# Two transformer blocks on one core: the gate of out_proj multiplied in from PSUM, affine steps behind the last tile, bias tables negated on ScalarE

## The chip, the core and the metric

The kernel runs on one core of a Trainium2 chip. The core has five engines with an instruction queue each, and each queue runs strictly in order: TensorE (PE) multiplies matrices into PSUM, VectorE (DVE) and ScalarE (ACT) work on tiles in SBUF and PSUM, GpSimd (POOL) on tiles in SBUF, and SyncE (SP) issues most of the DMAs. Engines wait for each other through semaphores. The metric is the device time of one execution in microseconds (us); lower is better. "Layer 0" and "layer 1" are the two layers of the second block.

## What is computed

Two transformer blocks run one after the other, all in float32. The first has 512 tokens of width 1024 and holds dilated attention, an mLSTM, cross attention and a mixture of experts; the change touches nothing there. The second block takes its output x (512 latent tokens) and 256 context tokens through two layers. Cut to what matters:

```python
for l in range(2):
    sh1, sc1, g1, sh2, sc2, g2 = split(silu(c) @ w_ada[l] + b_ada[l], 6)
    u = x * (1 + sc1) + sh1                # (the context has modulations of its own)
    o = concat(neighborhood_attention(u, bias from na_rpb[l]),   # 6 heads
               gated_linear_attention(u),                        # 4 heads, both directions
               gqa_attention(u))                                 # 6 query, 2 key heads
    x = layer_norm(ALPHA * x + g1 * (o @ w_out[l]), ln1_g[l], ln1_b[l])
    v = x * (1 + sc2) + sh2
    x = layer_norm(ALPHA * x + g2 * (silu(v @ wa) * (v @ wb)) @ w_ffn_out[l], ln2_g[l], ln2_b[l])
```

In the first layer the context goes through the same steps, ahead of the latent tokens. A layer_norm is a normalisation ((x - mean) / std) and an affine step (times ln_g, plus ln_b).

## The kernel before

Each float32 product is made of three matmuls: both operands are split into a high and a low part (names ending in _h and _l). A weight chunk of 256x512 or 1024x128 is loaded by SP into one of four buffers `raw`; ACT casts it to w_h (L350), DVE subtracts (L351) to get w_l, and PE multiplies it with the tokens (mm3, L343). Three split chunks (w) can stand ready. In places a chunk first takes a gate: `wchunk` with a `row` lets POOL multiply raw by it (L387).

The 512 latent tokens are four tiles of 128. A layer runs gated linear attention (GLA, with the decay tables glD made on POOL and exponentials on ACT), the projections, neighbourhood attention (NA), grouped-query attention (GQA), `out_proj` and `ffn`. In NA the keys of a head pair (nak) are duplicated by SBUF-to-SBUF DMAs (L533) before PE can make scores (sc, L542), and each head has a bias table `nab`, loaded by a DMA that POOL issues (L1621) and negated by POOL (L1622). Two nab buffers are used in turn.

`out_proj` multiplies the attention's output by W_out, gated by g1b on POOL, in two halves of 512 columns. DVE adds ALPHA * x (L2077) and takes the statistics (bn_stats, L2048). When a tile's second half is done, `done1` normalises it: `ln_moments` runs a reciprocal square root as a chain of one-column DVE instructions (L462 to L476, named rqv, rqz, rqa, rqb), DVE scales the tile (L2059), PE transposes it (tp, L500), ACT applies the modulation and casts (ht, hTf_h), DVE makes the low part (hTf_l, L515), and POOL brings x itself through the affine step for the residual (`affine`, L2066 and L2067: two instructions of 128x1024). ln_g and ln_b are folded into the modulation columns of the transposed copy, so that copy does not wait for POOL. `ffn` takes g2b into w_ffn_out on POOL (66 chunks, L387). Its last product ends tile by tile in `done2`, which is built like `done1` and in layer 0 also stores x to DRAM (xd, SP). In layer 1 `last` ends a tile: for tiles 0 to 2 DVE normalises and POOL does the affine step, for tile 3 DVE does all of it in three instructions (L2323, then L2326 twice) and the store goes out in halves.

The order of the instructions on each engine is set by the framework's scheduler, which simulates the queues while the program is built; memory of closed pools is reused behind semaphores. A change of one instruction can therefore move others on all engines, SP's queue among them. SP's DMAs carry semaphores in turn (DMAHW0 to DMAHW7), and one waits until the DMA that had the same one before has landed.

Of the kernel before, what the change touches and what calls it, by code (L numbers as in the profile page):

```python
# [9 lines left out]
F32 = mybir.dt.float32  # L10
# [5 lines left out]
OP = mybir.AluOpType  # L16
# [4 lines left out]
P = 128  # L21
D = 1024
KT = 8
T1 = 512
# [211 lines left out]
def f32(ap):  # L236
    return ap.bitcast(F32)
# [22 lines left out]
class Kern:  # L260
# [1351 lines left out]
    def na_bias(self, l, pool, bias):  # L1612

        h = len(bias)
        if h < NA_H:
            if h < 2:
                t = pool.tile([P, 4, 256], F32, name=f"nab{h}")
                self.nc.gpsimd.memset(t[:, 3, :], 0.0)
            else:
                t = bias[h - 2]  # L1620
            self.nc.gpsimd.dma_start(out=t[:, 0:3, :].rearrange("p a c -> p (a c)"), in_=self.A["nabias"][l, h])  # L1621
            self.nc.gpsimd.tensor_scalar_mul(t[:, 0:3, :], t[:, 0:3, :], -1.0)  # L1622
            bias.append(t)

    def na(self, l, hT, T, W, ctxd, full, d, vd, pool, pool0, g0, begun, bias):
# [430 lines left out]
    def ln_core(self, t, st):  # L2056

        m, r = self.ln_moments(st)
        self.nc.vector.tensor_scalar(out=t, in0=t, scalar1=m, scalar2=r, op0=OP.subtract, op1=OP.mult)  # L2059

    def call(self, f):
        if f is not None:
            f()
# [5 lines left out]
    def out_proj(self, l, oT, nt, x, g1b, pool, tile_done):  # L2069

        nc = self.nc
        W = self.A["w_out_2"][l]
        stats = {}

        def ev(i, c0, n, ps):
            s = slice(c0, c0 + n)
            nc.vector.scalar_tensor_tensor(out=x[:, i, s], in0=x[:, i, s], scalar=ALPHA, in1=ps[:, :n], op0=OP.mult, op1=OP.add)  # L2077
            self.ln_stats(stats, x, i, c0)
            if c0 + n == D:
                return tile_done(i, stats[i])  # L2080
        if nt < 4:
            return self.proj_tok(oT, nt, W, lambda *a: self.call(ev(*a)), row=g1b)
        self.proj_tok(oT, nt, W[:, 0:512], ev, row=g1b)
        self.proj_last(oT, nt, W, ev, pool, KT, g1b, (512,))

    def ffn(self, l, hT, T, x, g2b, pool, tile_done):

# [47 lines left out]
    def layer2(self, l, st, ctxd, full, last=None, keep_hT=False):  # L2135
# [3 lines left out]
        nt = T // P  # L2139
# [62 lines left out]
        with tpool("xx") as px:  # L2202
            x = px.tile([P, nt, D], F32, name="x")
            nc.sync.dma_start(out=x, in_=st["xd"].rearrange("(t p) d -> p t d", p=P))
            wk = px
            s, t = self.mod_cols(cols_, 4, 3, j, self.c("vpack", f"ln1_g{l}"), self.c("vpack", f"ln1_b{l}"), f"mc{j}", self.cst)
            hTf = self.hl_tile(px, [P, KT, T], "hTf")
            with tpool("l2") as lp:
                if not lat:
                    gr, lg, lb = ln_rows(lp)  # L2210

                def done1(i, stats):
                    self.ln_core(x[:, i, :], stats)

                    def rest():
                        self.hT_tile(x[:, i, :], i, hTf, s, t, lp, () if lat else (0, 2))
                        self.affine(x[:, i, :], x[:, i, :], lg, lb)
                    return rest
                self.out_proj(l, oT, nt, x, gr, wk, done1)
            oes.close()  # L2220
            st["hes"].close()
            with tpool("l3") as lp:
                gr = lp.tile([P, D], F32, name="g2b")
                self.ada_bcast(rows, 5, j, gr)
                lg, lb = (self.bcast_row(lp, r + 4 * l, n) if j == 0 else None for r, n in ((4, "lng"), (5, "lnb")))
                if last is None:
                    self.core_tile(st, nt)
                    hTn = st["hT"]
                    s2, t2 = self.mod_cols(st["ada"][l + 1][1], 1, 0, j, self.c("vpack", f"ln2_g{l}"),
                                           self.c("vpack", f"ln2_b{l}"), f"md{j}", self.cst)  # L2230

                    xd = self.dr.tile([T, D], F32, name=f"xd{l}{j}") if j == 0 else None

                def done2(i, stats):
                    if last is not None:
                        return last(i, x[:, i, :], stats, lg, lb)
                    self.ln_core(x[:, i, :], stats)

                    def rest():
                        self.hT_tile(x[:, i, :], i, hTn, s2, t2, lp, () if lat else (0, 2))  # L2240
                        if xd is not None:
                            self.affine(x[:, i, :], x[:, i, :], lg, lb)
                            nc.sync.dma_start(out=xd[i * P:(i + 1) * P, :], in_=x[:, i, :])
                    return rest
                self.ffn(l, lambda k: hTf[:, k, :], T, x, gr, wk, done2)
                if last is None:
                    st["xd"] = xd
        return d
# [18 lines left out]
    def main_stream(self):  # L2267
# [46 lines left out]

        def last(i, x, stats, g, b):
            rows = self.out[i * P:(i + 1) * P, :]
            if i < 3:
                self.ln_core(x, stats)
                self.affine(x, x, g, b)
                nc.sync.dma_start(out=rows, in_=x)  # L2320
                return
            m, r = self.ln_moments(stats)
            nc.vector.scalar_tensor_tensor(out=x, in0=x, scalar=m, in1=g, op0=OP.subtract, op1=OP.mult)  # L2323
            for c in range(0, D, 512):
# [26 lines left out]
```

## Time and profile before

| | us |
|---|---|
| three timed runs | 2722.61, 2729.33, 2729.94 (median 2729.33) |
| the profiled execution | 2717.65 |
| its span | 2715.8 |
| busy: PE / DVE / ACT / POOL | 2501.9 / 1747.8 / 1272.7 / 490.9 |

PE's granted clock is 0.96 of full speed over the span. The stages of the second block's latent tokens lie at these times of the span: GLA, projections and NA of layer 0 to about 1455, GQA to 1545, out_proj to 1603, FFN 0 to 1960, its norm and the start of layer 1 to 2000, NA of layer 1 at 2120 to 2195, GQA to 2270, out_proj to 2336, FFN 1 to 2690, the last norm to 2711.

How to read it: a row of a timeline has start, duration, engine, line, operation, the tile written and the tiles read; a bracket at its end tells how long the engine stood idle before and what ended that. An instruction's duration includes the time in which it is held up by another engine at memory. A table of windows gives each engine's busy time in a stretch.

### The profile page before, as it was taken

How to read it: one execution, taken by the hardware profiler on the slowest of the kernel's cores; microseconds unless marked ns; L12 is line 12 of the kernel's file. 1: busy time of each engine (PE TensorE's matmuls, PEld its weight loads, DVE VectorE, ACT ScalarE, POOL GpSimd, SP SyncE). 2: the span in 40 equal slices, each digit the busy share in tenths (PEclk: the TensorE clock that was granted, in tenths of full speed). 3: DMA queues.
4: the chain of work that ended last, by engine and by line, in shares of the span. 5: the costliest groups of instructions: out<-in, count | busy, mean ns of one | idle time of the engine just before them, and what ended most of it. 6: DMA issues, size and time to landing. Idle time of an engine off the chain costs nothing.

```text
span 2715.8 us, 35914 instructions
## 1 busy us (share of the span) xinstructions
PE 2501.9 (92%) x13176; PEld 1953.3 (72%) x13176; DVE 1747.8 (64%) x3095; ACT 1272.7 (47%) x2375; POOL 490.9 (18%) x335
## 2 busy tenths in 40 slices
PE   8999899898979999979988999999989789999997
PEld 5547575676658888867875588888778556888885
DVE  3346646887687787787777564444677676644446
ACT  4343444567755555556646532222356474422221
POOL 1100000201121111112223031111243220411103
PEclk9999899898989999989989999999989899999998
DMA  7765357589767888766352323333323424233331
GB/s 273 210 202 172 109 197 243 167 277 297 270 224 258 270 261 292 255 200 208 98 144 92 112 76 98 95 93 94 95 82 119 124 77 132 82 97 94 93 93 55
DMA packets 354723, 436.53 MB, mean 161 GB/s; under 512 B 20336, under 2 KB 228080, under 8 KB 354544
## 3 DMA queue, kind: packets, MB, share of 16 engines
q1 hardware_dynamic: 350128, 416.90, 48.7%
q0 software_dynamic: 4416, 17.30, 1.9%
q8 instruction: 105, 1.72, 0.3%
q14 instruction: 74, 0.61, 0.1%
HBM read 387.21 MB, written 38.01 MB: 157 GB/s over the span
## 4 chain that ended last, share of the span: by engine, by line
PE 52%; DVE 14%; DMA 5%; issue 5%; ACT 4%; POOL 1%; DVEq 0%; SPq 0%; ACTq 0%; POOLq 0%
PE fab L343 20%; PE pj L343 17%; DVE w_l L351 4%; PE pf L343 3%; PE oat L635 3%; PE h L343 3%; ACT w_h L350 2%; PE yps L343 2%; PE ptp L575 1%; DMA raw<-in_w 1%; DVE rqa L468 1%; PE sc L542 1%; DMA raw<-in_w_ffn_out 1%; POOL raw L387 1%; DMA nak_h<-nak_h 1%
## 5 line engine op out<-in xcount | busy, mean ns | idle before, releaser
L351 DVE TENSOR_TENSOR w_l<-raw,w_h 128x1024 fp32r<-128x1024 f32 (+2 forms) x530 | 696.3, 1325 | 451.5 <-ACT w_h L350 442.9
L350 ACT CAST w_h<-raw 128x1024 fp32r<-128x1024 f32 (+2 forms) x530 | 527.2, 1007 | 844.6 <-PE fab L343 271.0
L343 PE MATMUL fab<-hTf_l,w_h 128*128 128x512 f32 (+1 forms) x1104 | 386.6, 351 | 3.6 <-DVE hTf_l L515 3.6
L343 PE MATMUL fab<-hTf_h,w_h 128*128 128x512 f32 (+1 forms) x1104 | 385.9, 351 | 2.0 <-ACT hTf_h L514 1.7
L343 PE MATMUL fab<-hTf_h,w_l 128*128 128x512 f32 (+1 forms) x1104 | 386.5, 350 | 0.8 <-DVE w_l L351 0.7
L387 POOL TENSOR_TENSOR raw<-raw,g2b 128x1024 f32<-128x1024 f32 x66 | 171.0, 2595 | 756.8 <-DMA raw<-in_w_ffn_out 680.0
L343 PE MATMUL pj<-w_l,hT_h 128*128 128x512 f32 (+3 forms) x608 | 227.6, 375 | 9.9 <-DVE w_l L351 9.9
L343 PEld LDWEIGHTS fab<-hTf_l,w_h 128*128 128x128 f32 x1104 | 209.1, 189 | 35.7 <-DVE hTf_l L515 4.0
L343 PEld LDWEIGHTS fab<-hTf_h,w_h 128*128 128x128 f32 x1104 | 208.6, 189 | 35.3 <-ACT hTf_h L514 2.9
L343 PEld LDWEIGHTS fab<-hTf_h,w_l 128*128 128x128 f32 x1104 | 209.2, 189 | 33.4 <-DVE w_l L351 1.7
L343 PE MATMUL pj<-w_h,hT_h 128*128 128x512 f32 (+3 forms) x608 | 219.8, 374 | 10.4 <-ACT w_h L350 5.2
L343 PE MATMUL pj<-w_h,hT_l 128*128 128x512 f32 (+3 forms) x608 | 224.3, 371 | 0.0
L343 PE MATMUL pj<-w_h,wk_h 128*128 128x512 f32 x376 | 146.9, 396 | 6.1 <-DVE x L2096 4.5
L343 PE MATMUL pj<-w_l,wk_h 128*128 128x512 f32 x376 | 148.6, 396 | 1.2 <-DVE w_l L351 1.2
L343 PE MATMUL pj<-w_h,wk_l 128*128 128x512 f32 x376 | 145.8, 395 | 0.9 <-DVE wk_l L351 0.9
L343 PEld LDWEIGHTS pj<-w_h,hT_h 128*128 128x128 f32 x608 | 117.8, 196 | 38.4 <-ACT w_h L350 8.4
L343 PEld LDWEIGHTS pj<-w_l,hT_h 128*128 128x128 f32 x608 | 118.7, 195 | 36.8 <-DVE w_l L351 14.2
L343 PE MATMUL pf<-hT_h,w_h 128*128 128x512 f32 (+3 forms) x376 | 133.1, 355 | 9.1 <-DVE nak_l L351 4.0
L343 PEld LDWEIGHTS pj<-w_h,hT_l 128*128 128x128 f32 x608 | 119.1, 196 | 21.9 <-issue 5.4
L343 PE MATMUL pf<-hT_h,w_l 128*128 128x512 f32 (+3 forms) x376 | 130.8, 348 | 0.0
L343 PE MATMUL pf<-hT_l,w_h 128*128 128x512 f32 (+3 forms) x376 | 130.3, 347 | 0.0
L577 ACT COPY pT<-ptp 128x512 f32<-128x512 f32 (+3 forms) x184 | 88.5, 497 | 72.7 <-PE ptp L575 71.8
(594 smaller groups left out, 4928.1 us busy)
## 6 DMA issues: line engine op xcount, KB each, us to landing
raw<-in_w SPq DMA_DIRECT2D x192, 512.0 KB
raw<-in_w_ffn_in SPq DMA_DIRECT2D x132, 512.0 KB
raw<-in_w_ada SPq DMA_DIRECT2D x96, 512.0 KB
raw<-in_w_in SPq DMA_DIRECT2D x76, 512.0 KB
raw<-in_w_ffn_out SPq DMA_DIRECT2D x66, 512.0 KB
raw<-in_w_out SPq DMA_DIRECT2D x32, 512.0 KB
yd<-ysb SPq DMA_DIRECT2D x16, 512.0 KB
raw<-in_w_in SPq DMA_DIRECT2D x16, 384.0 KB
```

The lines of the kernel that those rows point to most:

```text
L343: self.nc.tensor.matmul(out, lhsT=l, rhs=r, start=first and k == 0 and i == 0, stop=last and k == n - 1 and i == 2, **kw)
L350: nc.scalar.copy(out=hl.hi, in_=src)
L351: nc.vector.tensor_sub(out=hl.lo, in0=src, in1=f32(hl.hi))
L387: self.nc.gpsimd.tensor_tensor(out=raw, in0=raw, in1=row.unsqueeze(1).to_broadcast([P, kt, n]), op=OP.mult)
L468: nc.vector.scalar_tensor_tensor(out=a, in0=z, scalar=v, in1=z, op0=OP.mult, op1=OP.mult)
L542: self.nc.tensor.matmul(o, lhsT=q, rhs=k.hi, start=True, stop=False)
L575: self.behind = nc.tensor.transpose(tp[:, b * P:(b + 1) * P], st["p"][:, (b0 + b) * P:][:, :P], self.ident)
L577: nc.scalar.copy(out=pT()[:, slice(b0, b0 + bb), ts], in_=tp[:, :bb * P].rearrange("p (b t) -> p b t", t=P))
L635: self.nc.tensor.matmul(st["o"][64 * hh:64 * hh + 64, cols_], lhsT=v(hh), rhs=pT(hh), start=n == 0, stop=n == len(terms) - 1, skip_group_c ...
```

## The change

- `na_bias`: the negation of the twelve nab tables moves from POOL to ACT.
- `out_proj` for the latent tokens: W_out is no longer multiplied by g1b on POOL. DVE multiplies the product by g1b from PSUM into a tile gps (128x512), and the residual add reads gps in place of PSUM.
- `done1` and layer 0's `done2`: the affine steps of the four latent tiles, and the stores to xd, no longer follow each tile. They are collected and issued behind a one-column POOL copy (bhd) that reads the last column of the last tile's low part, so that POOL starts them once the last tile is transposed and split.
- `last`: all four tiles now end on DVE, as tile 3 did, with stores in halves.

```diff
     def na_bias(self, l, pool, bias):
-            self.nc.gpsimd.tensor_scalar_mul(t[:, 0:3, :], t[:, 0:3, :], -1.0)
+            self.nc.scalar.mul(t[:, 0:3, :], t[:, 0:3, :], -1.0)
...
+    def behind_input(self, hT, pool, works):
+
+        t = pool.tile([P, 1], F32, name="bhd", tag="bhd", bufs=1)
+        with self.tc.issue_after(self.nc.gpsimd.tensor_copy(t, f32(hT.lo[:, KT - 1, T1 - 1:T1])).ins):
+            for f in works:
+                f()
...
         def ev(i, c0, n, ps):
             s = slice(c0, c0 + n)
+            if nt == 4:
+                t = pool.tile([P, 512], F32, name="gps", tag="gps", bufs=1)
+                nc.vector.tensor_tensor(out=t, in0=ps, in1=g1b[:, s], op=OP.mult)
+                ps = t
             nc.vector.scalar_tensor_tensor(out=x[:, i, s], in0=x[:, i, s], scalar=ALPHA, in1=ps[:, :n], op0=OP.mult, op1=OP.add)
...
-        self.proj_tok(oT, nt, W[:, 0:512], ev, row=g1b)
-        self.proj_last(oT, nt, W, ev, pool, KT, g1b, (512,))
+        self.proj_tok(oT, nt, W[:, 0:512], ev)
+        self.proj_last(oT, nt, W, ev, pool, KT, None, (512,))
...
-                        self.affine(x[:, i, :], x[:, i, :], lg, lb)
+                        later.append(lambda: self.affine(x[:, i, :], x[:, i, :], lg, lb))
+                        if not lat:
+                            later.pop()()
...
+                if lat:
+                    self.behind_input(hTf, lp, later)
...
-                            self.affine(x[:, i, :], x[:, i, :], lg, lb)
-                            nc.sync.dma_start(out=xd[i * P:(i + 1) * P, :], in_=x[:, i, :])
+                            later.append(lambda: keep_x(i))
...
+                def keep_x(i):
+                    self.affine(x[:, i, :], x[:, i, :], lg, lb)
+                    nc.sync.dma_start(out=xd[i * P:(i + 1) * P, :], in_=x[:, i, :])
...
+                if later:
+                    self.behind_input(st["hT"], lp, later)
...
         def last(i, x, stats, g, b):
             rows = self.out[i * P:(i + 1) * P, :]
-            if i < 3:
-                self.ln_core(x, stats)
-                self.affine(x, x, g, b)
-                nc.sync.dma_start(out=rows, in_=x)
-                return
             m, r = self.ln_moments(stats)
```

What this does to the queues is seen in the orders of the built programs. Names carry buffer numbers, and a bracket names the semaphores that an instruction waits for.

POOL in the norm behind FFN 0, before: from the last weight multiply on, each tile's multiply by ln_g (L2066) and add of ln_b (L2067).

```order
L387 TENSOR_TENSOR raw_18076<-raw_18076,g2b_15843 128x1024 [waits DMAHW7_49,DMAHW4_49,DVE_49]
L2066 TENSOR_TENSOR x_15397<-x_15397,lng_15846 128x1024 [waits DVE_49,PE_49]
L2067 TENSOR_TENSOR x_15397<-x_15397,lnb_15848 128x1024 [waits Pool_49]
L2066 TENSOR_TENSOR x_15397<-x_15397,lng_15846 128x1024 [waits DVE_49,PE_49] x2
L2067 TENSOR_TENSOR x_15397<-x_15397,lnb_15848 128x1024 [waits Pool_49] x2
```

POOL at the same place, now:

```order
L387 TENSOR_TENSOR raw_18086<-raw_18086,g2b_15853 128x1024 [waits DMAHW7_49,DMAHW4_49,DVE_49]
L2064 COPY bhd_18363<-hT_l_15864 128x1 [waits DMASW6_49,DVE_49]
L2073 TENSOR_TENSOR x_15397<-x_15397,lng_15856 128x1024 [waits PE_49] x4
L2074 TENSOR_TENSOR x_15397<-x_15397,lnb_15858 128x1024 [waits Pool_49] x4
L1737 TENSOR_TENSOR tcq_19611<-cpack_66,vpack_67 128x256
```

The pairs that were released tile by tile now stand as four multiplies and four adds behind bhd, and the tables of layer 1 (tcq and what follows) stand behind all eight.

SP in the neighbourhood attention of layer 1, before: the duplicated keys of the second head pair (nak), the context's values (navc) and the context's keys of the third (nakc).

```order
L1659 DMA navc_19864<-nav1256_12147 128x2x128 [waits DMAHW5_49]
L533 DMA nak_h_19866<-nak_h_19866 64x512 [waits DMAHW6_49,Activation_49]
L533 DMA nak_l_19867<-nak_l_19867 64x512 [waits DMAHW7_49,DVE_49]
L1659 DMA navc_20098<-nav1256_12147 128x2x128 [waits DMAHW0_49]
L533 DMA nak_h_19866<-nak_h_19866 64x512 [waits DMAHW1_49,Activation_49]
L533 DMA nak_l_19867<-nak_l_19867 64x512 [waits DMAHW2_49,DVE_49]
L375 DMA nakc_h_20370<-nakc12_h_12412 128x512 [waits DMAHW3_49,PE_49]
L375 DMA nakc_l_20372<-nakc12_l_12414 128x512 [waits DMAHW4_49,PE_49]
```

SP at the same place, now:

```order
L1659 DMA navc_19876<-nav1256_12147 128x2x128 [waits DMAHW5_49]
L533 DMA nak_h_19878<-nak_h_19878 64x512 [waits DMAHW6_49,Activation_49]
L1659 DMA navc_20110<-nav1256_12147 128x2x128 [waits DMAHW7_49]
L375 DMA nakc_h_20382<-nakc12_h_12412 128x512 [waits DMAHW0_49,PE_49]
L533 DMA nak_l_19879<-nak_l_19879 64x512 [waits DMAHW1_49,DVE_49]
L375 DMA nakc_l_20384<-nakc12_l_12414 128x512 [waits DMAHW2_49,PE_49]
L533 DMA nak_h_19878<-nak_h_19878 64x512 [waits DMAHW3_49,Activation_49]
L533 DMA nak_l_19879<-nak_l_19879 64x512 [waits DMAHW4_49,DVE_49]
```

The two nakc loads moved ahead of the second nak_h and nak_l, which now wait for DMAHW3 and DMAHW4.

ACT at the start of layer 1, before: casts of weight chunks (w_h), the first GLA products (glr, glq), the scaled queries of two groups (glqb) and the gates (gla_a).

```order
L350 CAST w_h_18580<-raw_18578 128x1024 [waits DMAHW1_49,PE_49]
L1840 COPY glr_18381<-pf_18400 32x512 [waits PE_49]
L350 CAST w_h_18610<-raw_18608 128x1024 [waits DMAHW2_49,PE_49]
L1868 ACTIVATE glq_18568<-pf_18401 128x512 [waits PE_49]
L1971 ACTIVATE glqb_18786<-glq_18568,cpack_66 128x2x128 [waits Activation_49,Pool_49]
L1971 ACTIVATE glqb_18786<-glq_18568,cpack_66 128x2x128 x2
L1971 ACTIVATE glqb_18800<-glq_18568,cpack_66 128x2x128 [waits DVE_49]
L1971 ACTIVATE glqb_18800<-glq_18568,cpack_66 128x2x128 x2
L350 CAST w_h_18640<-raw_18638 128x1024 [waits DMAHW3_49,PE_49]
L1850 ACTIVATE gla_a_18548<-glz_18550,vpack_67 128x512 [waits PE_49]
```

ACT at the same place, now:

```order
L350 CAST w_h_18592<-raw_18590 128x1024 [waits DMAHW1_49,PE_49]
L350 CAST w_h_18622<-raw_18620 128x1024 [waits DMAHW2_49,PE_49]
L350 CAST w_h_18652<-raw_18650 128x1024 [waits DMAHW3_49,PE_49]
L1840 COPY glr_18393<-pf_18412 32x512
L1868 ACTIVATE glq_18580<-pf_18413 128x512
L1971 ACTIVATE glqb_18798<-glq_18580,cpack_66 128x2x128 [waits Activation_49,Pool_49]
L1971 ACTIVATE glqb_18798<-glq_18580,cpack_66 128x2x128 x2
L1971 ACTIVATE glqb_18812<-glq_18580,cpack_66 128x2x128 [waits Pool_49]
L1971 ACTIVATE glqb_18812<-glq_18580,cpack_66 128x2x128 x2
L1850 ACTIVATE gla_a_18560<-glz_18562,vpack_67 128x512 [waits PE_49]
```

Three chunk casts now stand ahead of GLA's work, and both glqb groups wait for POOL: the counts in the built program are that of the fourth multiply for the first group and that of the fourth add for the second. The cast of the fourth chunk, which stood eight rows behind gla_a, now stands behind the decay tables' exponentials, where the cast of the fifth stood.

## Rows read from the trace of the kernel before

**Rows 1.** The page: busy time, share of the span and instructions by engine.
```profile
PE 2501.9 (92%) x13176; PEld 1953.3 (72%) x13176; DVE 1747.8 (64%) x3095; ACT 1272.7 (47%) x2375; POOL 490.9 (18%) x335
```
**Rows 2.** POOL's groups by shape: out<-in xcount | busy us, mean ns | idle before, releasers.
```profile
L387 POOL TENSOR_TENSOR raw<-raw,g1b 128x1024 f32<-128x1024 f32 x24 | 60.1, 2524 | 232.0 <-DMA raw<-in_w_out 152.8 <-DMA g1b<-adard 18.7 <-issue 15.8
L2067 POOL TENSOR_TENSOR x<-x,lnb 128x1024 f32<-128x1024 f32 x17 | 42.8, 2521 | 1.2
...
L1622 POOL TENSOR_SCALAR nab<-nab 128x768 f32<-128x768 f32 x12 | 26.9, 2249 | 47.9 <-DMA nab<-in_nabias 47.9
```
**Rows 3.** DVE timeline in the norm behind out_proj 0: start us, us, instruction.
```profile
1570.29 0.22 DVE L468 SCALAR_TENSOR_TENSOR rqa<-rqz,rqv 128x1 f32<-128x1 f32 x1
...
1571.38 0.81 DVE L2059 TENSOR_SCALAR x<-x,bmv,rqz 128x1024 f32<-128x1024 f32 x1
...
1577.23 2.25 DVE L468 SCALAR_TENSOR_TENSOR rqa<-rqz,rqv 128x1 f32<-128x1 f32 x1
```
**Rows 4.** POOL timeline of the same stretch: the second affine step of two tiles.
```profile
1577.06 2.40 POOL L2067 TENSOR_TENSOR x<-x,lnb 128x1024 f32<-128x1024 f32 x1
...
1584.43 2.40 POOL L2067 TENSOR_TENSOR x<-x,lnb 128x1024 f32<-128x1024 f32 x1
```
**Rows 5.** Windows: length, busy us by engine, PEclk, DMA share, GB/s.
```profile
1455.00:1490.00 35.00, 24.98 (x158) 16.76 (x156) 31.70 (x68) 25.14 (x64) 17.20 (x7) 0.90 0.33 109
1500.00:1545.00 45.00, 40.81 (x209) 23.39 (x208) 24.69 (x76) 27.94 (x82) 0.00 (x0) 1.00 0.20 64
...
2188.00:2220.00 32.00, 22.57 (x138) 14.79 (x132) 28.91 (x55) 21.38 (x53) 17.20 (x7) 0.84 0.31 102
...
1575.00:1603.00 28.00, 23.83 (x152) 20.81 (x151) 23.62 (x40) 14.84 (x38) 18.70 (x8) 1.00 0.08 19
1603.00:1940.00 337.00, 337.00 (x1471) 272.92 (x1470) 158.63 (x147) 90.97 (x109) 55.92 (x22) 0.99 0.34 101
```
**Rows 6.** PE timeline: the scores behind the duplicated keys, layer 0 and layer 1.
```profile
1421.69 0.55 PE L542 MATMUL sc<-nak_h,naq 128*128 128x256 f32 x1 [8.00 <-DMA nak_h<-nak_h]
...
2148.95 0.55 PE L542 MATMUL sc<-nak_h,naq 128*128 128x256 f32 x1 [12.61 <-DMA nak_h<-nak_h]
```
**Rows 7.** SP timeline in layer 1's neighbourhood attention: DMA issues.
```profile
2140.84 0.55 SPq L533 DMA_DIRECT2D nak_l<-nak_l  x1
...
2147.31 0.34 SPq L375 DMA_DIRECT2D nakc_l<-nakc_l  x1
```
**Rows 8.** PE's waits from 1575 to 1603: us in total, times, longest.
```profile
PE fab L343 <- DVE hTf_l L515: 1.8, 1, 1.8
PE tp L500 <- DVE x L2059: 1.7, 3, 0.8
```
**Rows 9.** PE's waits from 1958 to 1990.
```profile
PE tp L500 <- DVE x L2059: 10.8, 2, 5.9
```
**Rows 10.** DVE timeline behind FFN 0: first and last of five blocked instructions.
```profile
1960.14 2.00 DVE L473 SCALAR_TENSOR_TENSOR rqz<-rqa,rqz 128x1 f32<-128x1 f32 x1
...
1976.89 2.80 DVE L2059 TENSOR_SCALAR x<-x,bmv,rqz 128x1024 f32<-128x1024 f32 x1
```
**Rows 11.** ACT timeline at layer 1's start: the first glqb and the fifth chunk's cast.
```profile
1999.27 2.51 ACT L1971 ACTIVATE glqb<-glq,cpack 128x256 f32<-128x256 f32 x6
...
2015.91 1.03 ACT L350 CAST w_h<-raw 128x1024 fp32r<-128x1024 f32 x1
```
**Rows 12.** PE timeline there: the first products of the first and the fourth chunk.
```profile
2002.40 0.50 PE L343 MATMUL pj<-w_h,hT_h 128*128 128x512 f32 x1
...
2019.23 0.40 PE L343 MATMUL pj<-w_h,hT_h 128*128 128x512 f32 x1
```
**Rows 13.** DVE's groups from 2680 to 2716, the last norm.
```profile
L468 DVE SCALAR_TENSOR_TENSOR rqa<-rqz,rqv 128x1 f32<-128x1 f32 x8 | 10.2, 1280 | 0.2
...
L2323 DVE SCALAR_TENSOR_TENSOR x<-x,bmv,lng 128x1024 f32<-128x1024 f32 x1 | 2.5, 2549 | 0.0
...
L2326 DVE SCALAR_TENSOR_TENSOR x<-x,rqz,lnb 128x512 f32<-128x512 f32 x2 | 1.4, 750 | 0.0
```

More of the change, by code (lines that the diff above doesn't have):

```diff
@@ L2208, in layer2 @@
             with tpool("l2") as lp:
+                later = []
                 if not lat:
@@ L2241, in rest @@
                         if xd is not None:
-                            self.affine(x[:, i, :], x[:, i, :], lg, lb)
-                            nc.sync.dma_start(out=xd[i * P:(i + 1) * P, :], in_=x[:, i, :])
-                    return rest
+                            later.append(lambda: keep_x(i))
+                    return rest
+                def keep_x(i):
+                    self.affine(x[:, i, :], x[:, i, :], lg, lb)
+                    nc.sync.dma_start(out=xd[i * P:(i + 1) * P, :], in_=x[:, i, :])
+                later = []
                 self.ffn(l, lambda k: hTf[:, k, :], T, x, gr, wk, done2)
+                if later:
+                    self.behind_input(st["hT"], lp, later)
                 if last is None:
```

## The prediction

> **What bounds the kernel now.** The engine totals come first: TensorE (PE) is busy for 92% of the span, VectorE (DVE) for 64% [rows 1], so only PE's pauses can be won. POOL's groups tell what POOL does: the gate on W_out, the affine steps and the negated bias tables take 2.2 to 2.5 us an instruction, and the negations also waited 47.9 us for their loads [rows 2]. The DVE and POOL timelines show the coupling: one Newton step of the reciprocal root (L468) takes 0.22 us alone and 2.25 us where POOL's affine step of 2.40 us lies over it [rows 3, 4]. The stage table shows where PE pays [rows 5]. It is full for all of FFN 0, where POOL multiplies weights 22 times, and loses 4.2 us of 28 in the norm behind out_proj 0; layer 1 repeats that. In the 35 us in which layer 0's gate multiplies run, PE is busy for 71%, and for 91% in the attention right behind them; in layer 1's 32 us it is 71% too. So POOL costs time where DVE sets PE's pace, and nothing where PE is full.
>
> **Gate out of W_out.** 16 POOL instructions of 2.52 us go (of 24; the context's 8 stay) [rows 2]. If those 35 and 32 us ran at the later attention's 40.81 of 45, they would take 27.5 and 24.9 us: 7.5 and 7.1 us less is the upper bound [rows 5]. Not all of that idling is POOL's, since the windows also hold the change from one attention to the next; I take 2 a layer as the lower bound, a third of it. Nothing shows which end is nearer, so I take 5 each: **-10** (-4 to -14). W_out's casts now need no POOL and stand earlier on ScalarE (ACT) and DVE, inside neighbourhood attention, whose PE stalls below cover them. The gate returns as 16 DVE multiplies of 128x512 from PSUM, at most 0.75 us each by the two-input step of that shape [rows 13]; that is counted in the norm term.
>
> **Negation on ACT, and the queue that moves with it.** 12 multiplies of 128x768 on ACT cost at most a 128x1024 cast, 1.03 us [rows 11], by width 0.8: 9.5 us on an engine that is busy for 47% [rows 1]. ACT now also waits, in order, for the loads that POOL waited for; softmax exponentials and the casts of the keys (nak) are queued behind. What hides this are PE's two long stalls on the keys' duplicating DMAs, 8.0 us in layer 0 and 12.6 in layer 1 [rows 6], which lie behind such waits in each layer; without them each wait would cost what it lasts. I take 0 (to +3).
> The scheduler also reorders SP's queue. In layer 1 the loads nakc_h and nakc_l (256 KB each) now stand ahead of the second nak_h and nak_l. In the order listing those two take over the semaphore names DMAHW3 and DMAHW4 that the nakc loads had, so they wait for the same earlier transfers. The second nak_l was issued at 2140.84, nakc_l at 2147.31 [rows 7]; PE went on at 2148.95, when the keys had landed [rows 6]. So nak_l may go out 6.5 us later, with less traffic ahead of it: 0 to 6.5, of which I take the middle, 3. Layer 0 swaps one such load: 1 (0 to 2.5). Together **+4** (0 to 9).
>
> **The norm behind out_proj.** PE's waits there are 1.7 us for the normalised x in three pieces and 1.8 us for the last hTf_l [rows 8], within the 4.2 us of idling [rows 5]. With the affine steps behind the last tile, a tile loses about 2.2 us of blocked DVE time and gains a multiply of 0.75; DVE's period falls from the 7.4 us between two tiles' affine steps [rows 4] to some 5.9, just under PE's own 23.83 us for four tiles [rows 5]. What is late next is the last tile's transposes and casts, which stay: about 0.9 us. 4.2 - 0.9 = 3.3 a layer: **-6.6** (-3 to -8.4). The deferred run of 8 x 2.45 = 20 us then lies over FFN's start, beside its weight splits. What hides it is the ring of three split chunks, as it hides FFN 0's 22 POOL multiplies at 337 of 337 us [rows 5]; without that cover each split could wait 2.4 us.
> Here a rule speaks against the change. The Trainium skill (SBUF — State Buffer, Who interferes with whom) says that a VectorE instruction with two SBUF inputs contends with a GpSimd instruction that reads SBUF, and whichever comes second blocks for the whole instruction. Rows 3 and 4 agree, 0.22 against 2.25 us. By the rule the new residual add, which reads the gated product from SBUF and no longer from PSUM, becomes one more victim; with POOL empty there, the sum is the same by both.
>
> **The norm behind FFN 0, and layer 1's start.** Here PE waits 10.8 us for the normalised x [rows 9]. On the chain to the last x five DVE instructions are blocked; the first and the last take 2.00 and 2.80 us, all five 11.3 [rows 10], and alone they would take about 1.6 (four of 0.2, one of 0.8 [rows 3]): 9.7 us. But I do not book that. In the order listing ACT's second group of glqb, and DVE's, wait for POOL, by the built program's count for the last of the eight affine steps, since they reuse the affine rows' memory; behind them on ACT stand the gate activations, the decay's exponentials and the cast of the fourth weight chunk. Before, glqb at 1999.27 found POOL's steps long done [rows 11]. Now the last x ends near 1979.7 - 9.7 = 1970; its transposes, copies and splits take about 6 us (estimate), and 20 us of POOL end at 1996, or 1998 if DVE stretches them. The fourth cast stands where the fifth stood, 16.6 us behind glqb (2015.91 [rows 11]), so it runs at about 2013 to 2015, and PE has its chunk at about 2016. Before, PE began the first chunk at 2002.40 and the fourth at 2019.23 [rows 12]. It now comes to the fourth 9.7 us earlier, at 2009.5, and waits some 7 us: **-3**, nearest to the rows of ACT (+2 to -9.7).
> The reordered xd stores on SP wait for the same POOL steps; the fourth chunk's load stands ahead of them, and the loads behind are needed later.
>
> **The last norm.** After FFN 1 DVE alone sets the end; its chain is full from PE's last products on. Eight L468 take 10.2 us instead of 1.8, L2323 takes 2.5 instead of the 1.4 of two L2326 [rows 13], and three L2059 of 0.8 [rows 3] go: -11.9. Three tiles take on an L2323 and two halves, 3 x (1.4 + 1.4) = +8.4. **-3.5** (-2 to -5).
>
> **Sum.** -10 + 4 - 6.6 - 3 - 3.5 = -19.1 us: from the profiled execution's 2717.65 to 2698.6 (its span and the 1.9 us around it alike). That run lies 11.7 us under the median of the three timed runs, so the forecast takes the same step from the median: 2729.3 - 19.1 = **2710 us**. With the terms' bounds partly cancelling, its own range is 2702 to 2719.
>
> **Rivals.**
> - The wait for POOL does not bind (chance 0.20): the affine run ends sooner or PE has other work, and the FFN norm brings its 9.7. For it: PE's 10.8 us of waiting is real. Against it: the order of ACT. 2710 - 6.7 = 2703 us.
> - The attention is not held by POOL (0.22): its idle time is the change between the two attentions, and the gate brings 2 a layer. For it: the windows hold that change too. Against it: the two windows' equal 71% around the same POOL work. 2710 + 6 = 2716 us.
> - Slower (0.08): ACT takes over POOL's 47.9 us of waiting for the bias loads [rows 2] with the exponentials queued behind. If all but the two stalls of 8.0 and 12.6 us [rows 6] reaches PE, that is +27.3: 2710 + 27.3 = 2738 us. It turns the result from 19 us of uncovered waits on. Against it: ACT is busy for half of the time only, and the first two tables of a layer are loaded before the attention begins.
> - The forecast keeps 0.50.
>
> **How the numbers follow.** About 0.3% (8 us) is what a measurement of this kernel can tell from no change, so faster is below 2721 and slower above 2737. Forecast: 0.45 of its 0.50 below, the rest the same. First rival: 0.19 of 0.20 below. Second: 0.14 of 0.22 below, 0.07 the same, 0.01 slower. Third: slower. Faster 0.78, same 0.13, slower 0.09. The range leaves out the slow rival and the outer edges of the others: 2698 to 2723.
>
> **What would show it.** In the changed kernel's trace L468 should take 0.2 us behind out_proj and at the end, and PE's four us of idling behind out_proj should fall to one. The windows at the attention's start should show PE at 80% or more. At layer 1's start PE should idle some 7 us before the fourth weight chunk, with ACT waiting for POOL at glqb; if it does not, the first rival holds. The stall on nak in layer 1 should be 13 to 18 us long. Attention windows at 71% as before, or PE waiting on exponentials behind ACT's nab instructions, would make the prediction wrong.

## The result and the profile after

The changed kernel takes 2699.95 us (median of four runs, 2692.87 to 2709.36) against 2729.64 for the one before: ratio 0.9891, 95% interval 0.9861 to 0.9922, or 29.7 us less, where 19 were forecast. The profiled execution is the slowest of the four (2709.36, span 2707.6). Spans mislead here: the part ahead of GLA 0, in which PE runs the same instructions in the same order, takes 1286.9 us in this profile and 1268.5 in the one before. So lengths of stages are compared, each from one profiled execution, with limits read from PE's timeline: first neighbourhood score (sc), first grouped-query score, last attention product (oat), last transpose (tp), last product (fab).

| stage, us | before | changed | difference |
|---|---|---|---|
| GLA 0 (first glz to first sc) | 120.3 | 119.7 | -0.6 |
| attention 0: NA + GQA | 68.6 + 87.0 | 68.7 + 77.9 | -9.0 |
| out_proj 0 + FFN 0 (to last fab) | 398.0 | 395.7 | -2.3 |
| norm behind FFN 0 (to last tp) | 39.4 | 30.3 | -9.1 |
| start of layer 1 (to first sc) | 134.3 | 144.6 | +10.3 |
| attention 1: NA + GQA | 73.3 + 88.2 | 71.1 + 77.6 | -12.8 |
| out_proj 1 + FFN 1 | 396.5 | 399.0 | +2.5 |
| end | 41.7 | 36.1 | -5.6 |
| sum | 1447.3 | 1420.7 | -26.6 |

The page of the changed kernel answers [rows 1]: POOL lost 72 us of work, and PE has as many instructions as before, which took 13.5 us more in this profile.

```profile
PE 2515.4 (93%) x13176; PEld 1963.8 (73%) x13176; DVE 1725.2 (64%) x3117; ACT 1281.9 (47%) x2389; POOL 418.7 (15%) x304
```

**Attention.** Windows over GQA (length, busy us of PE, PEld, DVE, ACT, POOL, PEclk, DMA share, GB/s), layer 0 of the kernel before, and then both layers of the changed one:

```profile
1457.40:1544.40 87.00, 72.69 (x389) 43.44 (x387) 61.61 (x160) 57.81 (x160) 15.08 (x7) 0.96 0.21 68
```
```profile
1475.30:1553.20 77.90, 71.41 (x389) 43.40 (x388) 50.00 (x155) 54.58 (x158) 0.00 (x0) 0.98 0.17 58
2194.90:2272.50 77.60, 71.11 (x388) 43.02 (x386) 49.99 (x155) 54.59 (x157) 0.00 (x0) 0.98 0.18 57
```

POOL's 15.1 us are gone, DVE is busy for 11.6 us less, and the stage is 9.1 us shorter. DVE's groups by shape in layer 0's windows (count, busy us, mean ns, idle before) show which were blocked, before and changed:

```profile
L567 DVE TENSOR_SCALAR pga<-pga,rr 128x768 f32<-128x768 f32 x24 | 17.6, 731 | 0.3
L1553 DVE TENSOR_REDUCE nmx<-sc 128x1 f32<-128x512 f32 x24 | 16.4, 681 | 9.2 <-PE sc L543 9.2
L1558 DVE TENSOR_TENSOR nm<-nmx 128x1 f32<-128x1 f32 x24 | 6.4, 265 | 0.3
L567 DVE TENSOR_SCALAR pna<-pna,rr 128x512 f32<-128x512 f32 x4 | 5.6, 1397 | 0.0
...
L351 DVE TENSOR_TENSOR w_l<-raw,w_h 128x1024 fp32r<-128x1024 f32 x3 | 3.7, 1218 | 0.0
```
```profile
L1553 DVE TENSOR_REDUCE nmx<-sc 128x1 f32<-128x512 f32 x24 | 16.4, 684 | 10.8 <-PE sc L543 10.7
L567 DVE TENSOR_SCALAR pga<-pga,rr 128x768 f32<-128x768 f32 x24 | 14.7, 614 | 0.3
L1558 DVE TENSOR_TENSOR nm<-nmx 128x1 f32<-128x1 f32 x24 | 3.8, 156 | 0.4
L567 DVE TENSOR_SCALAR pna<-pna,rr 128x512 f32<-128x512 f32 x3 | 1.4, 480 | 0.0
```

The softmax scalings (L567), which work on SBUF alone, and the two-input maximum nm were held up, on the same instructions by 9.1 us in all (pga 2.8, nm 2.6, pna 3.7; 9.9 in layer 1). The other part of what DVE lost are three weight splits (L351), which were not held up: they left the window, since W_out's chunks no longer wait for POOL. PE's pauses tell the two apart. Of the 10.0 us that PE stood idle between 1457.4 and 1490 before, 8.7 lie in or right behind POOL's two runs of multiplies (1455.3 to 1465.1 and 1478.2 to 1485.6), and 0.8 beside the splits (1472.6 to 1478.3).

The reduction from PSUM (L1553) took 681 and 684 ns. The Trainium skill (SBUF — State Buffer, Who interferes with whom) says the same: `tensor_scalar` can take the port pair shared with GpSimd, `tensor_reduce` never contends on trn2. The trace agrees.

In the neighbourhood attention ACT now stands for the bias loads, and PE behind it. In layer 1 of the changed kernel ACT's row, and PE's wait for pna from 2123 to 2272 (1.9 us in all before):

```profile
2143.09 0.85 ACT L1622 ACTIVATE nab<-nab 128x768 f32<-128x768 f32 x1 [4.64 <-DMA nab<-in_nabias]
```
```profile
PE ptp L575 <- DVE pna L567: 5.6, 3, 2.7
```

**Norms.** Behind FFN 0, PE's wait of 10.8 us [rows 9] fell to the first row below (changed kernel, 1949 to 1980: us in total, times, longest). At the end DVE's groups (2671.5 to 2707.6) answer [rows 13]: eight L468 take 1.7 us instead of 10.2.

```profile
PE tp L500 <- DVE x L2059: 3.7, 2, 3.1
```
```profile
L2343 DVE SCALAR_TENSOR_TENSOR x<-x,rqz,lnb 128x512 f32<-128x512 f32 x8 | 5.6, 744 | 0.0
...
L2340 DVE SCALAR_TENSOR_TENSOR x<-x,bmv,lng 128x1024 f32<-128x1024 f32 x4 | 5.1, 1276 | 0.0
L468 DVE SCALAR_TENSOR_TENSOR rqa<-rqz,rqv 128x1 f32<-128x1 f32 x8 | 1.7, 213 | 0.1
```

### The profile page after: what moved, and what is told of

Read it like the earlier page. It is cut to its first block, busy times and chain, and to the rows that moved or that the text cites. A ratio compares the mean times of both kernels' runs of the same rounds, so it can differ in the third digit from the quotient of the medians.

```text
span 2707.6 us, 35926 instructions
## 1 busy us (share of the span) xinstructions
PE 2515.4 (93%) x13176; PEld 1963.8 (73%) x13176; DVE 1725.2 (64%) x3117; ACT 1281.9 (47%) x2389; POOL 418.7 (15%) x304
## 5 line engine op out<-in xcount | busy, mean ns | idle before, releaser
L351 DVE TENSOR_TENSOR w_l<-raw,w_h 128x1024 fp32r<-128x1024 f32 (+2 forms) x530 | 714.5, 1359 | 465.8 <-ACT w_h L350 456.6
L343 PE MATMUL pf<-hT_h,w_h 128*128 128x512 f32 (+3 forms) x376 | 133.4, 356 | 10.2 <-DVE nak_l L351 3.1
L343 PEld LDWEIGHTS pj<-w_h,hT_l 128*128 128x128 f32 x608 | 120.3, 198 | 22.0 <-issue 5.2
```

The source lines that it names most:

```text
L343: self.nc.tensor.matmul(out, lhsT=l, rhs=r, start=first and k == 0 and i == 0, stop=last and k == n - 1 and i == 2, **kw)
L351: nc.vector.tensor_sub(out=hl.lo, in0=src, in1=f32(hl.hi))
```

## Experiments

**Each part alone**, on the kernel before. Each kernel has one of five pieces of the diff shown above: the gate (with `gps`), the negation, the deferral in `done1`, that in `done2`, and `last`. Their first lines, in this order:

```diff
-        self.proj_tok(oT, nt, W[:, 0:512], ev, row=g1b)
+        self.proj_tok(oT, nt, W[:, 0:512], ev)
...
-            self.nc.gpsimd.tensor_scalar_mul(t[:, 0:3, :], t[:, 0:3, :], -1.0)
+            self.nc.scalar.mul(t[:, 0:3, :], t[:, 0:3, :], -1.0)
...
-                        self.affine(x[:, i, :], x[:, i, :], lg, lb)
+                        later.append(lambda: self.affine(x[:, i, :], x[:, i, :], lg, lb))
...
-                            self.affine(x[:, i, :], x[:, i, :], lg, lb)
+                            later.append(lambda: keep_x(i))
...
-            if i < 3:
-                self.ln_core(x, stats)
```

> The kernel before with one edit: the gate of out_proj multiplied in on DVE from PSUM. Stages are read on PE: the attention of a layer from its first scores of the neighbourhood attention to the last oat product (155.6 us in layer 0 and 161.5 in layer 1 before; 146.6 and 148.7 in the changed kernel). Theory (POOL's 16 weight multiplies held the attention): 145 to 149 and 147 to 152, PE busy for 90% or more where the first grouped-query scores run, out_proj's norm 1 us longer each for the 16 added DVE multiplies, which now run under POOL's affine steps; the whole 18 to 22 us shorter than before. Rival (the attention gained by the negation's move to ACT): both within 2 us of before, the whole within 4.

> The kernel before with one edit: the twelve nab tables negated on ACT. Theory (the gate made the gain): the attention stages within 3 us of 155.6 and 161.5, with PE idle for 7 us or more before the scores of the second key pair; the whole within 5 us of before. Rival (the negation, off POOL and with other work ahead of those scores on PE, made the gain): 147 and 149 us, the whole 18 to 22 us shorter.

> The kernel before with one edit: the affine steps behind out_proj deferred behind the last tile, the gate still on POOL. Theory (the deferral frees DVE, and in the changed kernel the gate's DVE multiplies took the gain back): the stretch from the last oat product to the last transposed tile falls from 52.2 us to 49 to 50 in each layer, L468 takes 0.2 us there, and the whole is 4 to 7 us shorter. Rival (the waits of PE there are not DVE's, so the deferral brings nothing): 52 us as before, the whole within 3 us.

> The kernel before with one edit: the affine steps and stores behind FFN 0 deferred behind the last tile. Theory (layer 1's start gives the gain back, since ACT's scaled queries wait for the last affine step): from the end of FFN 0's first products to the last transposed tile 39.4 us become 29 to 31, from there to the first scores of layer 1 134.3 become 143 to 145, ACT waits 4 to 8 us for POOL at L1971; the whole within 3 us of before. Rival (the wait for POOL does not reach PE): the second stretch stays at 134 to 136, the whole is 8 to 10 us shorter.

> The kernel before with one edit: all four tiles of the last norm end on DVE. Theory: from the end of the last products to the end 41.7 us become 36 to 38, and the whole is 4 to 6 us shorter. Rival (POOL's steps ran beside DVE's chain and cost little): 40 to 42 us, the whole within 2.

| stage, us | before | gate | negation | out_proj norm | FFN norm | last |
|---|---|---|---|---|---|---|
| attention 0 | 155.6 | 147.6 | 156.0 | 157.4 | 155.6 | 155.5 |
| attention 1 | 161.5 | 147.7 | 155.0 | 165.3 | 161.2 | 162.3 |
| out_proj + FFN, both layers | 794.5 | 805.9 | 794.6 | 784.7 | 795.1 | 793.3 |
| norm behind FFN 0 | 39.4 | 39.4 | 39.4 | 39.4 | 30.4 | 39.3 |
| start of layer 1 | 134.3 | 133.1 | 133.2 | 133.0 | 145.2 | 133.8 |
| end | 41.7 | 41.7 | 41.6 | 41.7 | 41.6 | 36.2 |
| sum with GLA 0, against before | | -11.6 | -7.7 | -5.5 | +2.1 | -6.3 |
| time, ratio (95%) | | 0.9964 (0.9952 to 0.9976) | 0.9956 (0.9940 to 0.9973) | 0.9952 (0.9934 to 0.9970) | 0.9995 (0.9978 to 1.0012) | 0.9960 (0.9943 to 0.9978) |

The five stage sums add up to -29.0, near the changed kernel's -26.6. The times add up to -47 (0.36 + 0.44 + 0.48 + 0.05 + 0.40% of 2730), each with some 5 us of uncertainty; sizes are therefore taken from the stages. What remains of the difference lies ahead of GLA 0, where nothing is changed and the profiles start GLA 0 at 1268.5 to 1289.7 us; its cause is open.

- **Gate**: both attentions came out as expected, but the whole gained half: out_proj and FFN take 11.4 us more, out_proj's stretch alone 4.9 and 5.2 where 1 each was expected. GQA is 10.7 and 12.1 us shorter: PE idles 7.8 and 7.7 us less in it, and its busy time falls from 72.7 and 74.0 to 69.8 and 69.6 us, with the granted clock at 1.00 instead of 0.96 and 0.94 (layer 0's window below). DVE's two steps a half tile now lie under POOL's affine steps; x<-x,gps took 1.11 us on average there, and 0.69 in the changed kernel.
- **Negation**: neither theory. Attention 0 stood still as the first said; attention 1 fell by 6.5, and the time by 12 (7.7 by the stages). In layer 1 20 products of a projection chunk now run ahead of the scores that wait for the duplicated keys, and the stall there is 5.1 us instead of 12.6.
- **out_proj norm**: out_proj fell from 52.2 to 50.0 and 49.9, FFN behind it by 3.3 and 2.0 us: 9.8 us in both layers, more than the 4 to 7 expected. Of PE's waits there only the first fence below is left. Attention 1 was 4 us longer in this one profile, unexplained.
- **FFN norm**: as expected, no gain. ACT waited 6.8 us for POOL at glqb.
- **Last**: 5.5 us at the end, as expected.

GQA of layer 0 with the gate alone, in the columns of the windows above:

```profile
1467.80:1544.10 76.30, 69.79 (x389) 42.72 (x387) 50.06 (x155) 54.65 (x157) 0.00 (x0) 1.00 0.17 59
```

PE's waits in out_proj's norm of layer 0 (us in total, times, longest): out_proj norm alone, gate alone, and changed. Before it was 4.2: the 3.5 of [rows 8], and 0.7 for hTf_h.

```profile
PE fab L343 <- ACT hTf_h L514: 0.7, 1, 0.7
```
```profile
PE tp L500 <- DVE x L2059: 4.7, 3, 2.2
PE fab L343 <- DVE hTf_l L515: 2.6, 2, 1.8
PE fab L343 <- ACT hTf_h L514: 1.5, 1, 1.5
```
```profile
PE tp L500 <- DVE x L2059: 2.2, 1, 2.2
PE fab L343 <- ACT hTf_h L514: 1.5, 1, 1.5
```

So the deferral took 3.5 of the 4.2 us a layer, and the gate on DVE brought 3.0 back.

**Parts taken back from the changed kernel**: the gate, the negation and the deferral in `done2`, each by its piece of the diff reversed. The first lines:

```diff
-        self.proj_tok(oT, nt, W[:, 0:512], ev)
+        self.proj_tok(oT, nt, W[:, 0:512], ev, row=g1b)
...
-            self.nc.scalar.mul(t[:, 0:3, :], t[:, 0:3, :], -1.0)
+            self.nc.gpsimd.tensor_scalar_mul(t[:, 0:3, :], t[:, 0:3, :], -1.0)
...
-                            later.append(lambda: keep_x(i))
+                            self.affine(x[:, i, :], x[:, i, :], lg, lb)
```

> The changed kernel with W_out gated on POOL again. Its order on PE in layer 1 has the waiting scores ahead of the projection chunk, as before. Theory (the gate holds DVE in the grouped-query attention, and the order of that chunk the layer's start): from the first grouped-query scores to the last oat product 87 to 89 us in each layer instead of 77.9 and 77.6, layer 1's attention with a stall of 10 us or more on the duplicated keys and about 160 us in all; out_proj's stretch 50 us; the whole 10 to 15 us slower than the changed kernel. Rival (the parts overlap and the gate is no more than half of the attention's gain): 5 us slower at most.

It took 2710.66 us, ratio 0.9919 (0.9891 to 0.9947): 7.6 us over the changed kernel by the ratios, between the two forecasts, and 6.0 by the stages (1426.7 against 1420.7). Attention is 7.1 and 11.6 us longer (GQA 86.9 and 86.8), out_proj and FFN 11.6 shorter. Its SP queue has the nakc loads ahead of the second nak pieces as the changed kernel's has, but PE has the waiting scores ahead of the next projection chunk, as before. PE's scores behind the duplicated keys in layer 1 (start, us; in brackets the idle time before and what ended it), here and then in the changed kernel, with the chunk's first product:

```profile
2143.29 0.55 PE L542 MATMUL sc<-nak_h,naq 128*128 128x256 f32 x1 [6.65 <-DMA nak_h<-nak_h]
...
2146.45 0.58 PE L543 MATMUL sc<-nak_l,naq 128*128 128x256 f32 x1 [2.60 <-DMA nak_l<-nak_l]
```
```profile
2150.01 0.79 PE L343 MATMUL pf<-hT_h,w_h 128*128 128x512 f32 x1 [0.97 <-ACT pT L577]
...
2159.15 0.38 PE L543 MATMUL sc<-nak_l,naq 128*128 128x256 f32 x1 [1.92 <-DMA nak_l<-nak_l]
```

SP issued the second nak_l of the changed kernel late (start, us), as forecast:

```profile
2155.09 0.47 SPq L533 DMA_DIRECT2D nak_l<-nak_l  x1
```

But in the changed kernel 20 products of that chunk run ahead of the first of these scores, with two transposes (ptp) between; in the one before, none. Where they do, PE works while the keys travel. The negation does not settle that order by itself: alone on the kernel before it came with it, here, beside the deferrals, it did not.

> The changed kernel with the nab tables negated on POOL again. Theory (what the negation alone brought in layer 1 is that a projection chunk stands ahead of the waiting scores on PE, and the gate's move brings the same order by itself): the attention stages stay at 146 to 149 us, the whole within 3 us of the changed kernel. Rival (the negation's gain is its own, POOL's time beside DVE): attention 3 to 6 us longer in each layer, the whole 8 to 12 slower than the changed kernel.

2701.95 us, ratio 0.9885 (0.9860 to 0.9909) against the changed kernel's 0.9891, so the whole is the same; attention 149.6 and 146.9. The negation has nothing of its own in layer 1: alone it came with the chunk's order, which the gate's move brings too. In layer 0 it has 3 us, nearer to the rival: with the tables on POOL again PE stands 6.9 us for the keys, where it stands 0.5 in the changed kernel, and NA takes 71.6 us instead of 68.7 (71.3 with the gate alone).

> The changed kernel with one edit taken back: the affine steps and stores behind FFN 0 follow each tile again. Theory (layer 1's start gives the deferral's gain back): the norm takes 39 us instead of 30.3 and the stretch from there to layer 1's first scores 134 instead of 144.6, the whole within 3 us of the changed kernel, 27 to 33 under the one before. Rival (with the gate gone the deferral pays): 7 to 10 us slower than the changed kernel.

2696.91 us, 0.9880 (0.9852 to 0.9908): the same as the changed kernel. The norm is 39.4 again and the start of layer 1 133.4. The stages are 6.6 us less in all, 4.1 of it in the attention, which this edit does not touch: stages of single profiles can differ by that much.

**Two repairs.** First the run of affine steps on DVE; `behind_input` then anchors them to a DVE copy:

```diff
-                    self.affine(x[:, i, :], x[:, i, :], lg, lb)
+                    for r, op in ((lg, OP.mult), (lb, OP.add)):
+                        nc.vector.tensor_tensor(out=x[:, i, :], in0=x[:, i, :], in1=r, op=op)
...
-                    self.behind_input(st["hT"], lp, later)
+                    self.behind_input(st["hT"], lp, later, nc.vector)
```

> The changed kernel with the eight affine steps behind FFN 0 on DVE in place of POOL, still behind the last tile. Theory (what gives the gain back is POOL's 22 us, which ACT's scaled queries wait for): the norm stays at 30 to 31 us, ACT no longer waits at L1971 for more than 1 us, the stretch to layer 1's first scores falls from 144.6 to 136 to 139, the whole is 6 to 9 us under the changed kernel, 35 to 40 under the one before. Rival (it is the scheduler's order there, or DVE, now 10 us longer at work ahead of its weight splits, that holds PE): 143 to 147 us, the whole within 3 us of the changed kernel.

2695.09 us, 0.9857 (0.9832 to 0.9881). The start of layer 1 takes 137.3 us instead of 144.6. In the changed kernel POOL's run lasts to 2006.4, ACT's second glqb waits for it, and PE then for chunks (POOL's timeline, one row for four instructions; ACT's and PE's waits, 1979 to 2040; windows):

```profile
1984.66 9.45 POOL L2073 TENSOR_TENSOR x<-x,lng 128x1024 f32<-128x1024 f32 x4
1994.04 12.39 POOL L2074 TENSOR_TENSOR x<-x,lnb 128x1024 f32<-128x1024 f32 x4
```
```profile
ACT glqb L1971 <- POOL x L2074: 6.5, 1, 6.5
```
```profile
PE pj L343 <- DVE w_l L351: 3.4, 3, 1.7
PE pj L343 <- ACT w_h L350: 2.3, 1, 2.3
```
```profile
1979.20:2002.00 22.80, 20.77 (x159) 19.03 (x156) 12.90 (x9) 9.87 (x20) 17.48 (x8) 0.98 0.24 75
2002.00:2020.00 18.00, 18.00 (x59) 12.72 (x60) 9.65 (x12) 13.39 (x20) 9.50 (x14) 0.81 0.58 191
2020.00:2040.00 20.00, 16.34 (x63) 12.56 (x63) 15.99 (x23) 11.45 (x26) 6.20 (x5) 0.83 0.17 46
```

With the affine steps on DVE ACT no longer waits for POOL there, and PE not for chunks; the same stretch by windows:

```profile
1976.80:2002.00 25.20, 25.20 (x174) 22.66 (x172) 17.24 (x20) 11.74 (x24) 0.00 (x0) 0.94 0.51 181
2002.00:2020.00 18.00, 17.87 (x77) 13.75 (x75) 12.19 (x16) 17.17 (x26) 2.40 (x3) 1.00 0.24 64
2020.00:2040.00 20.00, 16.31 (x98) 12.76 (x99) 16.39 (x32) 9.51 (x24) 6.50 (x4) 1.00 0.10 25
```

PE idles 5.7 us in the changed kernel and 3.8 here; in these rows the larger part of the difference is the clock. Behind an idle piece of 1.7 us at 2000 and around later ones of 2.3 and 1.3, PE was granted 0.81 and 0.83 of full speed, a mix of 1.2 and 2.4 GHz: 18 x 0.19 + 20 x 0.17 + 22.8 x 0.02 = 7.3 us of full-speed work less, against 25.2 x 0.06 = 1.5 here. Some 0.7 of the 7.3 fall on time in which PE idled anyway. The two differences, 1.9 and 5.1, then come to 7.0 of the 7.3 us of the stage. Idling alone does not tell the clock, though: the last window here idles 3.7 us at 1.00. In the kernel before, PE ran through at this row and then at 1.00:

```profile
1981.80:2002.00 20.20, 20.20 (x148) 18.51 (x146) 11.67 (x10) 9.74 (x21) 10.25 (x13) 0.90 0.42 133
```

The lower clock ahead of the fourth chunk did not set the stage's length, though: PE would have stood longer for that chunk's cast. The kernel of the second repair below has the same affine steps on POOL and was granted 1.00 from 1976 to 2015; there PE waited 5.55 us for the cast in place of 2.34, and the stage takes 144.7 us, as in the changed kernel. With the affine steps on DVE the cast starts 34.3 us behind the last transpose, with them on POOL 43.2. PE's first product of the fourth chunk, in the changed kernel and in that of the second repair:

```profile
2023.49 1.20 PE L343 MATMUL pj<-w_h,hT_h 128*128 128x512 f32 x4 [2.34 <-ACT w_h L350]
```
```profile
2016.95 1.65 PE L343 MATMUL pj<-w_h,hT_h 128*128 128x512 f32 x3 [5.55 <-ACT w_h L350]
```

The second repair fixes one order in out_proj:

```diff
-                nc.vector.tensor_tensor(out=t, in0=ps, in1=g1b[:, s], op=OP.mult)
+                with self.tc.issue_after(self.scaled.ins) if i and c0 + n == D else ExitStack():
+                    nc.vector.tensor_tensor(out=t, in0=ps, in1=g1b[:, s], op=OP.mult)
```

> The changed kernel with one order fixed in out_proj: the gate multiply of a tile's second half (L2087) is issued on DVE behind the scaling of the tile before (L2059), so that DVE does not stand at the head of its queue for PE's products while PE waits for that scaling. Theory (the 2.2 us that PE waits there in each layer come from this order): the wait is gone, the stretch from the last oat product to the last transposed tile falls from 53.1 and 55.1 us to 50 to 52, and the whole is 3 to 6 us under the changed kernel, 33 to 36 under the one before. Rival (the gate's multiplies are simply too many for DVE, and the wait moves to the next tile): 53 to 55 us as now, the whole within 2 us of the changed kernel.

2695.79 us, 0.9860 (0.9832 to 0.9888); out_proj 50.8 and 51.0 instead of 53.1 and 55.1. DVE's timeline in the changed kernel, and PE's row that waited for it:

```profile
1582.42 0.69 DVE L2086 TENSOR_TENSOR gps<-pj,g1b 128x512 f32<-128x512 f32 x1 [1.41 <-PE pj L343]
1583.03 0.15 DVE L476 SCALAR_TENSOR_TENSOR rqz<-rqb,rqz 128x1 f32<-128x1 f32 x1
1583.15 0.69 DVE L2088 SCALAR_TENSOR_TENSOR x<-x,gps 128x512 f32<-128x512 f32 x1
1583.76 0.81 DVE L2059 TENSOR_SCALAR x<-x,bmv,rqz 128x1024 f32<-128x1024 f32 x1
```
```profile
1584.62 1.09 PE L500 MATMUL tp<-cpack,x 128*128 128x128 f32 x8 [2.24 <-DVE x L2059]
```

The first tile's chain was one instruction short (L476) when DVE stood at the head of its queue for the second tile's product. With the scaling first, DVE and PE read:

```profile
1575.37 0.16 DVE L476 SCALAR_TENSOR_TENSOR rqz<-rqb,rqz 128x1 f32<-128x1 f32 x1
1575.57 0.81 DVE L2059 TENSOR_SCALAR x<-x,bmv,rqz 128x1024 f32<-128x1024 f32 x1
1576.76 0.69 DVE L2087 TENSOR_TENSOR gps<-pj,g1b 128x512 f32<-128x512 f32 x1 [0.38 <-PE pj L343]
```
```profile
1576.56 1.04 PE L500 MATMUL tp<-cpack,x 128*128 128x128 f32 x8
```

By the ratios the two repairs are 9 and 8 us under the changed kernel, with overlapping intervals; the stages that they touch show 7.3 us for the first, and for the second 6.4 in out_proj, of which FFN gives 1.7 back. Both together:

> The changed kernel with both repairs: the affine steps behind FFN 0 on DVE behind the last tile, and in out_proj the gate multiply of a tile's second half behind the scaling of the tile before. Theory (the two gains lie in different stretches and add): out_proj's stretch 50 to 51.5 us in both layers, layer 1's start 136 to 139, the whole 38 to 42 us under the one before, 9 to 12 under the changed kernel. Rival (a new order elsewhere, or the same slack counted twice): 34 to 36 under the one before.

2682.98 us, ratio 0.9824 (0.9800 to 0.9848): 48 us under the kernel before. By the ratios it is 18 us under the changed kernel, more than the 9 to 12 expected; the stages show 15.3 (1405.4 against 1420.7), of which out_proj 6.3 (51.1 and 50.8), the start of layer 1 6.5 (138.1) and attention 2.2. This version is better than both kernels.

## Why the prediction was right, and where it was not

The time lies in the stated range of 2698 to 2723, 10 us below the forecast of 2710 and just under that forecast's own 2702 to 2719. The terms erred more than the sum, in both directions, so that the sum came this close is in part luck.

- **Gate out of W_out (-10 forecast).** Mechanism right, size short: attention gained 21.8 us with the gate alone, and lost 18.7 when it was taken back. The upper bound of 7.5 and 7.1 was no bound, since it took PE's busy time in the two windows as fixed, while those windows were granted 0.90 and 0.84 of full speed [rows 5]. As an estimate, with all of PE's time taken to follow the clock, 24.98 and 22.57 us become 22.5 and 19.0 at full speed, and at the later attention's 40.81 of 45 these take 24.8 and 20.9: 10.2 and 11.1 us less, 21.3 in all. The gate alone shows both parts in GQA: 15.5 us less idling and 7.3 us less busy time (the neighbourhood attention gave 0.9 back). DVE's rows fit, with 9.1 and 9.9 us of blocked time.
- **The gate's multiplies on DVE ("counted in the norm term").** This step failed. They cost 11.4 us over both layers with the affine steps beside them, and 11.6 by the kernel with the gate taken back. The forecast compared DVE's period a tile with PE's; what counted was DVE's order, which put the next tile's multiply ahead of the last step of the first tile's chain. With that order alone put right, 6.4 us came back in out_proj, 4.7 with FFN; the rest was not taken apart. The norm behind out_proj was forecast at -6.6 with the multiplies in; out_proj and FFN together show +0.2.
- **Negation and SP's queue (+4).** The DMA step held: the second nak_l went out 31.3 us after the layer's first score instead of 24.7, and the first score on it ran 35.4 instead of 33.2 us after it, 2.2 later for a forecast of 3 [rows 7]. But the expected stall of 13 to 18 us became 1.9, since PE's own order had moved; only SP's had been read. ACT's waits for the bias loads were hidden as forecast, though they reached PE: ACT stood 4.6 us for a table ahead of the exponentials of pna, and PE's transposes then 2.7 and 0.8 us for pna (1.2 and 0.8 in layer 0). That lay where PE had stood for the keys; the first of these scores ran 33.1 us after the layer's first, against 32.9 before [rows 6]. Together with the gate, layer 1's NA is 2.2 us shorter.
- **Norm behind FFN 0 and the start of layer 1 (-3).** The norm gained 9.1 of the 9.7 booked, and ACT waited for POOL at glqb as forecast. PE had the fourth chunk 44.3 us behind the last transpose (at 2023.49), 37.4 before (2019.23 [rows 12]): 6.9 us later, for a forecast of 7, though PE idled only 4.4 of them and ran the rest at the lower clock. What the forecast lacks comes behind that product: 3.4 us more to the first scores, in which PE waits 1.3 us for a split (w_l) and is granted 0.57 from 2023.5 to 2031.5, where the kernel before was granted 1.00. Together that is the +10.3 of the stage, and +1.2 with the norm's gain. The rival in which the wait does not bind is out.
- **The last norm (-3.5).** -5.6: L2340 took 1.28 us and the halves 0.74, so the three added tiles cost 3 x (1.28 + 1.49) = 8.3, as booked. DVE's rows account for 4.1 us (L468 -8.5, L2059 -2.4, the new form +6.8); of the other 1.5, 0.8 lie behind DVE's last instruction (4.8 us to the end before, 4.0 now), and 0.7 were not traced.
- **Rivals.** Attention not held by POOL: refuted by GQA's 77.9 and 77.6 us. ACT's waits for the bias loads (+27.3): they reached PE with 1.9 us in layer 0 and 3.4 in layer 1, where it had stood for the keys before. The signs named for the attention came out mixed: PE is busy for 92% at its start (26.4 of 28.7 us), and it does wait on exponentials behind ACT's nab instructions, which was named as a sign against the forecast.

## What to carry to other kernels

When work is moved between engines, read the order of the engine that waits as well as that of the queue it waits for: whether a stall costs anything is decided by what stands behind it on PE. Price contention on the victim's rows (busy time of the same instructions with and without the neighbour) rather than by scaling idle windows, mind that PE's busy time itself shrinks when its clock comes back (though a lower clock cost nothing where PE only ran towards a chunk that was not ready), and price the work's new place with the order that it stands in on that engine at its first tile. Deferred work whose buffers are reused hands its time on to whoever takes that memory, so put it on the engine that ends it soonest.

## What the runs showed of the hardware

- The eight affine steps behind FFN 0 took 21.8 us on POOL (2.36 us a multiply and 3.10 an add) and 9.2 on DVE (1.22 us each, L2263), with POOL idle. Beside POOL's run three weight splits on DVE took 3.37 us each; at the same place of the kernel before they took 1.23.
- One wait of 2.2 us cost different amounts: out_proj took 53.1 us in layer 0 and 55.1 in layer 1 with the same waits, and in layer 1 the 13 us around the wait (2298.5 to 2311.5) show a granted clock of 0.87 where layer 0's show 1.00. With the deferral behind FFN 0 taken back both layers take 53.2 us.

DVE's splits beside POOL's run (changed, 1990 to 2003), and in the kernel before (1994 to 2004):

```profile
L351 DVE TENSOR_TENSOR w_l<-raw,w_h 128x1024 fp32r<-128x1024 f32 x3 | 9.9, 3366 | 7.4 <-ACT w_h L350 7.4
```
```profile
L351 DVE TENSOR_TENSOR w_l<-raw,w_h 128x1024 fp32r<-128x1024 f32 x3 | 3.7, 1226 | 9.1 <-ACT w_h L350 9.1
```
